# A two-layer hybrid backbone: table products on VectorE, sign folded into the product, table stores on other queues

## The chip, the cores and the metric

The kernel runs on one core of a Trainium2 chip. The metric is device microseconds (us) of one execution. Lower is better. Three runs of the kernel before gave 2425.04, 2426.26 and 2430.54 us, a median of 2426.26 us.

## The reference, cut to what matters

The model has two layers. Each runs a SwiGLU feed-forward block, four parallel token mixers on one normalised input, and a second feed-forward block; each block is normalised and modulated by vectors that come from a conditioning input. All of it is float32, over 256 latent and 256 context tokens of 1024 channels, with a hidden width of 2816.

```python
def swiglu(h, w1, w3, w2):
    return (jax.nn.silu(h @ w1) * (h @ w3)) @ w2

# one of the four mixers: a complex diagonal state space model, per group of 16 channels, 64 states
a_re, a_im, bb_re, bb_im = s5_discretize(lam_re[dr], lam_im[dr], log_dt[dr], b_re[dr], b_im[dr])
x_ctx = complex_scan(a_re, a_im, einsum('gpn,blgn->blgp', bb_re, ug_ctx), ..., None, rev)
x_lat = complex_scan(a_re, a_im, ..., (x_ctx[0][:, end], x_ctx[1][:, end]), rev)
y_lat = y_lat + (einsum('gnp,blgp->blgn', c_re[dr], x_lat[0])
                 - einsum('gnp,blgp->blgn', c_im[dr], x_lat[1]))
```

The state space mixer depends on the layer's parameters in two ways: through powers of the complex decay `a`, and through products of these powers with `bb` (the input map) and `c` (the output map). The kernel works these products out once per layer, as tables, and keeps them in DRAM until the mixer reads them.

## The kernel before

**The main stream.** Nearly all matmuls are float32 made of three float32r matmuls (`mm3`, L345 to L347): high part times high part, high times low, low times high. A weight piece is 128 x 1024. `piece` (L323) loads it into `raw` by a DMA on SP's queue (L326); ScalarE copies it to the high part `whi` (L317), VectorE subtracts to give the low part `wlo` (L318). `raw` has three buffers, `whi` and `wlo` four each. In a feed-forward block `up` runs 24 matmuls of 128 x 512 on one piece. After every second piece `act` (L681 to L688) makes the activation: `t` on ScalarE, `gf` on VectorE (L686), `gh` on ScalarE (L687), `gl` on VectorE (L688).

**Beside it.** While a feed-forward block runs, two generators are stepped along, 0.6 steps to a weight piece (`pace`). One is `ada` (L401), the modulation vectors: it loads pieces `araw` into the same three `raw` buffers, and VectorE reduces them with two vectors `cr` (L424, four instructions to a piece). The other is `s5_tables` (L1252), the tables of one layer. The tables of layer 0 run beside the first block of layer 0 (some 75 to 420 us of the span), those of layer 1 beside the second block of layer 0 (some 1060 to 1340 us). They are read by the mixers, some 400 us and more after they are stored.

**The tables.** After 16-wide arithmetic on VectorE, a loop over direction `d` and half `hf` (4 turns, L1347) makes two complex products of 128 x 512: `v` (powers times `bb`) and `g` (powers times `c`), each by `cmul` (L1214), which is six `tensor_tensor` instructions. Both run on GpSimd, and so does one `tensor_scalar` that flips the sign of g[1] (L1364). The two `g` go to DRAM table G by DMAs on SP's queue (L1367). `turned` (L1336) transposes the `v` of the turn before on TensorE (L1341), four 128 x 128 blocks into a PSUM bank of tag "f" (3 buffers), has ScalarE copy it out as `s5vt` (L1342), and stores it to table V on SP's queue (L1343). Matmuls of `g` give table K (16 small stores, L1411), from which DRAM copies make W (8, L1414); rotations R (4, L1450) and Z (2, L1451) end the tables. All of these stores, too, are on SP's queue. The counts are for one layer.

**The order.** A tile scheduler fixes one order of instructions for each engine and each queue; `behind` gives the tables a later priority than the main stream. An engine, and SP's queue, goes through its instructions strictly in that order: one that waits holds up all behind it.

Of the kernel before, what the change touches and what calls it, by code (L numbers as in the profile page):

```python
# [11 lines left out]
ALU = mybir.AluOpType  # L12
# [4 lines left out]
D = 1024  # L17
# [169 lines left out]
class Kern:  # L187
# [1023 lines left out]
        return t  # L1211


    def cmul(self, o, x, y, t, eng=None):  # L1214

        e = eng or self.nc.vector
        e.tensor_tensor(t[0], x[0], y[0], op=ALU.mult)
        e.tensor_tensor(t[1], x[1], y[1], op=ALU.mult)
        e.tensor_tensor(o[0], t[0], t[1], op=ALU.subtract)
        e.tensor_tensor(t[0], x[0], y[1], op=ALU.mult)  # L1220
        e.tensor_tensor(t[1], x[1], y[0], op=ALU.mult)
        e.tensor_tensor(o[1], t[0], t[1], op=ALU.add)

    def exp_small(self, x, sm):

# [26 lines left out]
    def s5_tables(self, l):  # L1252
# [3 lines left out]
        nc, vec, act = self.nc, self.nc.vector, self.nc.scalar  # L1256
# [73 lines left out]

        ncim = self.u("s5nc")
        vec.tensor_scalar(ncim[:, :256], ct[:, 256:], -1.0, None, op0=ALU.mult)
        D = self.s5_dram[l]
        G, held = {}, []

        def turned(d, hf, v):  # L1336

            for ri in range(2):
                pt, vt = self.ps("s5vt", "f"), self.u("s5vt")
                for a in range(4):  # L1340
                    nc.tensor.transpose(pt[:, a * P : (a + 1) * P], v[ri][:, a * P : (a + 1) * P], self.ident)  # L1341
                act.copy(vt, pt)  # L1342
                nc.sync.dma_start(D["V"][d, ri, hf], vt)  # L1343
                yield


        for d in range(2):  # L1347
            for hf in range(2):
                o = slice(8 * d + 4 * hf, 8 * d + 4 * hf + 4)
                shp = [P, 4, 8, 16]  # L1350
                v4 = lambda t: t.rearrange("p (a j m) -> p a j m", a=4, j=8)
                bcv = lambda x: x[:, o].unsqueeze(2).to_broadcast(shp)

                def pwv(rev, lo):
                    w = [p[:, o, lo : lo + 8] for p in pw]
                    return [(x[:, :, ::-1] if rev else x).unsqueeze(3).to_broadcast(shp) for x in w]

                ta, tb = self.u("s5ta"), self.u("s5tb")
                v = [self.u("s5v"), self.u("s5v")]
                self.cmul([v4(x) for x in v], [bcv(x) for x in bb], pwv(d == 0, 0), (v4(ta), v4(tb)), nc.gpsimd)  # L1360
                yield
                g = [self.u("s5g"), self.u("s5g")]
                self.cmul([v4(x) for x in g], [bcv(x) for x in c3_], pwv(d == 1, 1), (v4(ta), v4(tb)), nc.gpsimd)
                nc.gpsimd.tensor_scalar(g[1], g[1], -1.0, None, op0=ALU.mult)  # L1364
                for ri in range(2):
                    G[d, ri, hf] = g[ri]
                    nc.sync.dma_start(D["G"][d, ri, hf], g[ri])  # L1367
                yield
                if held:
                    yield from turned(*held.pop())  # L1370
                held.append((d, hf, v))
# [4 lines left out]
        for ri in range(2):  # L1376
            t = self.u("s5bd")
# [9 lines left out]
        for hf in range(2):  # L1387
            ps = self.ps("s5k", "f")
            seen = set()

            def mm(o, d, ri, rhs, stop):
                for q in range(4):
                    r = rhs(q)
                    nc.tensor.matmul(ps[32 * q : 32 * q + 32, o : o + r.shape[-1]], bd[ri][:, 8 * d + 4 * hf + q], r,
                                     start=q not in seen, stop=stop, tile_position=(0, 32 * q), skip_group_check=True)
                    seen.add(q)

            for d in range(2):
                for ri in range(2):
                    lo, c = (0, 128) if d == 0 else (16, 0)  # L1400
                    mm(c, d, ri, lambda q: G[d, ri, hf][:, q * P + lo : q * P + lo + 112], ri == 1)
            for d in range(2):
                mm(112, d, 0, lambda q: c3_[0][:, 8 * d + 4 * hf + q], False)
                mm(112, d, 1, lambda q: ncim[:, (8 * d + 4 * hf + q) * 16 : (8 * d + 4 * hf + q) * 16 + 16], d == 1)
            kt = self.u("s5k")
            act.copy(kt[:, :240], ps[:, :240])
            vec.tensor_tensor(kt[:, 112:128], kt[:, 112:128], dsk[:, 16 * hf : 16 * hf + 16], op=ALU.add)
            for q in range(4):
                for par in range(2):
                    r = 32 * q + 16 * par  # L1410
                    nc.sync.dma_start(D["K"][:, 4 * hf + q, 240 * par : 240 * par + 240], kt[r : r + 16, :240])  # L1411
            yield
        for s in range(8):
            nc.sync.dma_start(  # L1414
                D["W"][s], D["K"].rearrange("m a (b j) -> m (a b) j", b=2)[:, :, 16 * (7 - s) : 16 * (7 - s) + 128])

        rt = [sm("r8") for i in range(4)]
# [10 lines left out]
        for d in range(2):  # L1428
# [18 lines left out]
            vec.tensor_copy(zv, m8[:, o].unsqueeze(2).to_broadcast([P, 8, 64]))  # L1447
            vec.memset(zv[:, :, 0:1], 0.0)
            for i in range(2):
                nc.sync.dma_start(D["R"][d, i], rot[i])  # L1450
            nc.sync.dma_start(D["Z"][d], z)  # L1451

    def s5_in(self, l, H, tag):
        nc, vec, act, mm = self.nc, self.nc.vector, self.nc.scalar, self.nc.tensor.matmul
# [363 lines left out]
```

## Time and profile before

| | before |
|---|---|
| median of three runs | 2426.26 us |
| the profiled execution | 2430.84 us |
| its span, first to last instruction | 2429.1 us |
| TensorE busy (PE) | 2278.5 us, 94% |
| VectorE busy (DVE) | 1641.2 us, 68% |
| ScalarE busy (ACT) | 902.7 us, 37% |
| GpSimd busy (POOL) | 166.4 us, 7% |
| mean granted TensorE clock | 0.972 |

Times inside the trace are us from the span's start. An engine's row gives start, duration, engine, line, operation, output and input; a bracket gives the idle time before it and what ended that. A row of SP (SPq) is a DMA's issue, not the transfer. "PE idle" means no matmul ran. The digits that give the granted clock are shares of full speed: 1.00 is 2.4 GHz, and in a stretch at half it is 1.2 GHz.

### The profile page before, as it was taken

The numbers are of one execution on the slowest core, as the hardware profiler recorded it, in microseconds if no ns is written. First come the engines' busy times: TensorE is split into PE (matmuls) and PEld (weight loads), VectorE is DVE, ScalarE is ACT, GpSimd is POOL, SyncE is SP. The second block draws the span as 40 slices with busy tenths as digits, with TensorE's granted clock in tenths as the row PEclk, the third lists the DMA queues.
The fourth block names the chain that finished last, engine by engine and source line by source line (L and its number), as shares of the span: only waits on it lengthen the run. The fifth ranks groups of instructions, "written<-read, shape, count | busy, mean of one in ns | idle before, by whom it ended". The sixth has DMA issues, their size and how long they took to land.

```text
span 2429.1 us, 39327 instructions
## 1 busy us (share of the span) xinstructions
PE 2278.5 (94%) x15428; PEld 1923.3 (79%) x15428; DVE 1641.2 (68%) x3929; ACT 902.7 (37%) x1551; POOL 166.4 (7%) x144
## 2 busy tenths in 40 slices
PE   7969989999999999988799999999998999998997
PEld 4757878987667777887677898888898887898997
DVE  5876566766565565799665558868757787678554
ACT  3313323363443323442222233323234664345443
POOL 0093000000000000006510000000000000000000
PEclk9989999999999999999899999999998999998999
DMA  7526454232441242233454423656542332354663
GB/s 237 180 90 183 155 170 156 73 94 77 132 161 41 86 150 83 79 122 120 149 166 158 135 86 117 204 177 196 173 139 81 109 109 69 122 187 134 186 184 114
DMA packets 111226, 326.84 MB, mean 135 GB/s; under 512 B 16256, under 2 KB 23168, under 8 KB 111040
## 3 DMA queue, kind: packets, MB, share of 16 engines
q1 hardware_dynamic: 109024, 320.65, 42.8%
q10 hardware_dynamic: 2016, 3.67, 0.5%
q8 instruction: 121, 1.98, 0.3%
q14 instruction: 65, 0.53, 0.1%
HBM read 311.20 MB, written 15.17 MB: 134 GB/s over the span
## 4 chain that ended last, share of the span: by engine, by line
PE 73%; DVE 14%; DMA 6%; ACT 3%; issue 2%; POOL 2%; SPq 0%; DVEq 0%; ACTq 0%; POOLq 0%
PE h L345 8%; PE h L347 8%; PE h L346 8%; PE y L345 5%; PE y L347 5%; PE y L346 5%; PE pj L345 5%; PE pj L347 5%; PE pj L346 5%; DMA araw<-in_w_adaT_dram 3%; DVE wlo L318 3%; DVE aj L424 2%; DMA raw<-in_ffn_dram 2%; PE s L841 2%; DVE araw L424 1%
## 5 line engine op out<-in xcount | busy, mean ns | idle before, releaser
L317 ACT CAST whi<-raw 128x1024 fp32r<-128x1024 f32 x402 | 421.1, 1050 | 843.0 <-DMA raw<-in_ffn_dram 308.8
L318 DVE TENSOR_TENSOR wlo<-raw,whi 128x1024 fp32r<-128x1024 f32 x402 | 499.5, 1245 | 302.9 <-ACT whi L317 300.3
L347 PE MATMUL h<-hh,wlo 128*128 128x512 f32 (+1 forms) x1472 | 529.8, 361 | 22.1 <-DVE wlo L318 22.1
L345 PE MATMUL h<-hh,whi 128*128 128x512 f32 (+1 forms) x1472 | 531.2, 362 | 16.8 <-DVE gf L686 11.2
L346 PE MATMUL h<-hl,whi 128*128 128x512 f32 (+1 forms) x1472 | 528.3, 360 | 0.0
L347 PEld LDWEIGHTS h<-hh,wlo 128*128 128x128 f32 x1472 | 283.4, 193 | 67.7 <-DVE wlo L318 24.7
L345 PEld LDWEIGHTS h<-hh,whi 128*128 128x128 f32 x1472 | 284.1, 193 | 62.0 <-issue 12.1
L346 PEld LDWEIGHTS h<-hl,whi 128*128 128x128 f32 x1472 | 284.0, 193 | 39.2
L345 PE MATMUL y<-gh,whi 128*128 128x256 f32 (+1 forms) x902 | 290.3, 322 | 2.6 <-ACT t L685 2.6
L347 PE MATMUL y<-gh,wlo 128*128 128x256 f32 (+1 forms) x902 | 290.8, 323 | 0.0
L346 PE MATMUL y<-gl,whi 128*128 128x256 f32 (+1 forms) x902 | 290.5, 322 | 0.0
L345 PE MATMUL pj<-hh,whi 128*128 128x256 f32 (+1 forms) x800 | 276.5, 348 | 3.3 <-ACT hh L565 2.7
L347 PE MATMUL pj<-hh,wlo 128*128 128x256 f32 (+1 forms) x800 | 274.5, 345 | 3.5 <-DVE wlo L318 3.5
L346 PE MATMUL pj<-hl,whi 128*128 128x256 f32 (+1 forms) x800 | 275.4, 346 | 0.0
L345 PEld LDWEIGHTS y<-gh,whi 128*128 128x128 f32 x902 | 171.7, 190 | 15.7 <-ACT t L685 2.8
L346 PEld LDWEIGHTS y<-gl,whi 128*128 128x128 f32 x902 | 171.7, 190 | 13.0
L347 PEld LDWEIGHTS y<-gh,wlo 128*128 128x128 f32 x902 | 171.7, 190 | 12.8
L345 PEld LDWEIGHTS pj<-hh,whi 128*128 128x128 f32 x800 | 154.1, 194 | 23.6 <-issue 5.2
L347 PEld LDWEIGHTS pj<-hh,wlo 128*128 128x128 f32 x800 | 153.9, 193 | 23.6 <-DVE wlo L318 4.8
L346 PEld LDWEIGHTS pj<-hl,whi 128*128 128x128 f32 x800 | 154.2, 193 | 18.4 <-issue 3.9
L424 DVE SCALAR_TENSOR_TENSOR aj<-araw,cr 128x512 f32<-128x512 f32 x112 | 89.8, 802 | 81.8 <-DMA araw<-in_w_adaT_dram 80.1
L687 ACT CAST gh<-gf 128x512 fp32r<-128x512 f32 (+1 forms) x88 | 49.8, 565 | 161.4 <-DVE gf L686 160.0
(391 smaller groups left out, 3188.3 us busy)
## 6 DMA issues: line engine op xcount, KB each, us to landing
raw<-in_ffn_dram SPq DMA_DIRECT2D x267, 512.0 KB, 3.8
araw<-in_w_adaT_dram SPq DMA_DIRECT2D x104, 512.0 KB, 4.1
raw<-in_win_dram SPq DMA_DIRECT2D x102, 512.0 KB, 3.7
araw<-in_w_ada_dram SPq DMA_DIRECT2D x24, 512.0 KB, 4.0
raw<-in_wout_dram SPq DMA_DIRECT2D x17, 512.0 KB, 3.5
raw<-in_wbr_dram SPq DMA_DIRECT2D x16, 512.0 KB, 3.7
araw<-in_w_ada_dram SPq DMA_DIRECT2D x22, 256.0 KB, 5.9
s5G<-s5g SPq DMA_DIRECT2D x16, 256.0 KB, 4.5
```

Of the source, the lines that this page charges most:

```text
L317: self.nc.scalar.copy(hi, src)
L318: self.nc.vector.tensor_tensor(lo, src, hi.bitcast(F32), op=ALU.subtract)
L345: mm(ps, wh, xh, start=start, stop=False, skip_group_check=True)
L346: mm(ps, wh, xl, start=False, stop=False, skip_group_check=True)
L347: mm(ps, wl, xh, start=False, stop=stop, skip_group_check=True)
L424: nc.vector.scalar_tensor_tensor(w if v else junk, w, 1.0, S[v], op0=ALU.mult, op1=ALU.mult, accum_out=t[:, 2 * op + i, v : v + 1])
L687: nc.scalar.copy(gh[:, a:b], gf[:, a:b])
L841: nc.tensor.matmul(s[:, :w], q[:, j * P : (j + 1) * P], k[:, :w], start=True, stop=True)
```

## The change

`cmul` takes a further operand `nxi`, the negated imaginary part; with it the last product is written with its sign flipped, by a subtraction in place of the addition, so that the separate sign change is no longer needed. The negated part exists already as `ncim`. The `v` and `g` products run on VectorE. The stores of G, K, W, R and Z are issued by GpSimd, those of V by ScalarE right behind its own copy.

```diff
--- before.py
+++ after.py
@@ -1211,15 +1211,18 @@
         return t
 
 
-    def cmul(self, o, x, y, t, eng=None):
+    def cmul(self, o, x, y, t, eng=None, nxi=None):
 
         e = eng or self.nc.vector
         e.tensor_tensor(t[0], x[0], y[0], op=ALU.mult)
         e.tensor_tensor(t[1], x[1], y[1], op=ALU.mult)
         e.tensor_tensor(o[0], t[0], t[1], op=ALU.subtract)
         e.tensor_tensor(t[0], x[0], y[1], op=ALU.mult)
-        e.tensor_tensor(t[1], x[1], y[0], op=ALU.mult)
-        e.tensor_tensor(o[1], t[0], t[1], op=ALU.add)
+        e.tensor_tensor(t[1], x[1] if nxi is None else nxi, y[0], op=ALU.mult)
+        if nxi is None:
+            e.tensor_tensor(o[1], t[0], t[1], op=ALU.add)
+        else:
+            e.tensor_tensor(o[1], t[1], t[0], op=ALU.subtract)
 
     def exp_small(self, x, sm):
 
@@ -1330,6 +1333,7 @@
 
         ncim = self.u("s5nc")
         vec.tensor_scalar(ncim[:, :256], ct[:, 256:], -1.0, None, op0=ALU.mult)
+        nci = ncim[:, :256].rearrange("p (a m) -> p a m", m=16)
         D = self.s5_dram[l]
         G, held = {}, []
 
@@ -1340,7 +1344,7 @@
                 for a in range(4):
                     nc.tensor.transpose(pt[:, a * P : (a + 1) * P], v[ri][:, a * P : (a + 1) * P], self.ident)
                 act.copy(vt, pt)
-                nc.sync.dma_start(D["V"][d, ri, hf], vt)
+                act.dma_start(D["V"][d, ri, hf], vt)
                 yield
 
 
@@ -1357,14 +1361,13 @@
 
                 ta, tb = self.u("s5ta"), self.u("s5tb")
                 v = [self.u("s5v"), self.u("s5v")]
-                self.cmul([v4(x) for x in v], [bcv(x) for x in bb], pwv(d == 0, 0), (v4(ta), v4(tb)), nc.gpsimd)
+                self.cmul([v4(x) for x in v], [bcv(x) for x in bb], pwv(d == 0, 0), (v4(ta), v4(tb)))
                 yield
                 g = [self.u("s5g"), self.u("s5g")]
-                self.cmul([v4(x) for x in g], [bcv(x) for x in c3_], pwv(d == 1, 1), (v4(ta), v4(tb)), nc.gpsimd)
-                nc.gpsimd.tensor_scalar(g[1], g[1], -1.0, None, op0=ALU.mult)
+                self.cmul([v4(x) for x in g], [bcv(x) for x in c3_], pwv(d == 1, 1), (v4(ta), v4(tb)), None, bcv(nci))
                 for ri in range(2):
                     G[d, ri, hf] = g[ri]
-                    nc.sync.dma_start(D["G"][d, ri, hf], g[ri])
+                    nc.gpsimd.dma_start(D["G"][d, ri, hf], g[ri])
                 yield
                 if held:
                     yield from turned(*held.pop())
@@ -1408,10 +1411,10 @@
             for q in range(4):
                 for par in range(2):
                     r = 32 * q + 16 * par
-                    nc.sync.dma_start(D["K"][:, 4 * hf + q, 240 * par : 240 * par + 240], kt[r : r + 16, :240])
+                    nc.gpsimd.dma_start(D["K"][:, 4 * hf + q, 240 * par : 240 * par + 240], kt[r : r + 16, :240])
             yield
         for s in range(8):
-            nc.sync.dma_start(
+            nc.gpsimd.dma_start(
                 D["W"][s], D["K"].rearrange("m a (b j) -> m (a b) j", b=2)[:, :, 16 * (7 - s) : 16 * (7 - s) + 128])
 
         rt = [sm("r8") for i in range(4)]
@@ -1447,8 +1450,8 @@
             vec.tensor_copy(zv, m8[:, o].unsqueeze(2).to_broadcast([P, 8, 64]))
             vec.memset(zv[:, :, 0:1], 0.0)
             for i in range(2):
-                nc.sync.dma_start(D["R"][d, i], rot[i])
-            nc.sync.dma_start(D["Z"][d], z)
+                nc.gpsimd.dma_start(D["R"][d, i], rot[i])
+            nc.gpsimd.dma_start(D["Z"][d], z)
 
     def s5_in(self, l, H, tag):
         nc, vec, act, mm = self.nc, self.nc.vector, self.nc.scalar, self.nc.tensor.matmul
```

By the built programs, VectorE has 3569 rows and had 3473: 96 products of 128 x 512, 48 in each layer. GpSimd loses these 96 and 8 sign changes, and gains the DMA issues; what it still computes is the clearing of tiles. SP has 680 rows and had 730.

The first place is SP's queue in layer 0, at the first two turns of the loop (`raw` and `araw` are weight pieces, `s5g` the products on their way to table G). Before:

```order
L326 DMA raw_1325<-in_ffn_dram 128x1024
L1367 DMA s5G_90<-s5g_1063 128x512
L1367 DMA s5G_90<-s5g_1064 128x512
L326 DMA raw_1356<-in_ffn_dram 128x1024
L420 DMA araw_1362<-in_w_adaT_dram 128x1024
L1367 DMA s5G_90<-s5g_1197 128x512
L1367 DMA s5G_90<-s5g_1198 128x512
L326 DMA raw_1409<-in_ffn_dram 128x1024
L420 DMA araw_1415<-in_w_adaT_dram 128x1024
```

Now:

```order
L326 DMA raw_1323<-in_ffn_dram 128x1024
L326 DMA raw_1354<-in_ffn_dram 128x1024
L420 DMA araw_1360<-in_w_adaT_dram 128x1024
L326 DMA raw_1407<-in_ffn_dram 128x1024
L420 DMA araw_1413<-in_w_adaT_dram 128x1024
L326 DMA raw_1454<-in_ffn_dram 128x1024
L326 DMA raw_1493<-in_ffn_dram 128x1024
```

The four stores have left SP's queue, and the loads that stood behind them follow one another directly.

The second place is VectorE at the same time, up to the first weight piece after the products have begun (`s5ta`, `s5tb` are the products' temporaries, `s5bb` and `s5c` the maps, `s5s` small tables; the piece's name ends in 1244 before and in 1242 now). Before:

```order
L1219 TENSOR_TENSOR s5s_659<-s5s_658 128x16
L1220 TENSOR_TENSOR s5s_658<-s5s_659 128x16
L1221 TENSOR_TENSOR s5s_658<-s5s_659 128x16
L688 TENSOR_TENSOR gl_1046<-gf_1044,gh_1045 128x512
L1222 TENSOR_TENSOR s5s_659<-s5s_658 128x16
L1217 TENSOR_TENSOR s5s_658<-s5s_659 128x16
L1218 TENSOR_TENSOR s5s_658<-s5s_659 128x16
L1219 TENSOR_TENSOR s5s_659<-s5s_658 128x16
L1220 TENSOR_TENSOR s5s_658<-s5s_659 128x16
L1221 TENSOR_TENSOR s5s_658<-s5s_659 128x16
L1222 TENSOR_TENSOR s5s_659<-s5s_658 128x16
L318 TENSOR_TENSOR wlo_1244<-raw_1241,whi_1243 128x1024
```

Now, from the first product on; the row ahead of it, a gl, stands twelve rows ahead of the part shown of before:

```order
L1217 TENSOR_TENSOR s5ta_977<-s5bb_922,s5s_658 128x512
L1218 TENSOR_TENSOR s5tb_978<-s5bb_922,s5s_659 128x512
L424 SCALAR_TENSOR_TENSOR aj_651,mod_3_642<-araw_1276,cr_645 128x512
L1219 TENSOR_TENSOR s5v_979<-s5ta_977,s5tb_978 128x512
L424 SCALAR_TENSOR_TENSOR araw_1276,mod_3_642<-araw_1276,cr_648 128x512
L1220 TENSOR_TENSOR s5ta_977<-s5bb_922,s5s_659 128x512
L1221 TENSOR_TENSOR s5tb_978<-s5bb_922,s5s_658 128x512
L424 SCALAR_TENSOR_TENSOR aj_651,mod_3_642<-araw_1276,cr_645 128x512
L1223 TENSOR_TENSOR s5v_980<-s5ta_977,s5tb_978 128x512
L686 TENSOR_TENSOR gf_1044<-t_1043,h_1018 128x512
L424 SCALAR_TENSOR_TENSOR araw_1276,mod_3_642<-araw_1276,cr_648 128x512
L318 TENSOR_TENSOR wlo_1242<-raw_1239,whi_1241 128x1024
```

The six instructions of the first `v` product stand among the main stream's; the 16-wide instructions stand later, and the piece's `wlo` comes before the second `gl`.

The third place is VectorE at the end of the tables of layer 0, where the second K tile is finished (`s5k`). The bracket lists the semaphores that a row waits for; those that begin with DMAHW belong to DMAs issued by SP or ScalarE, those with DMASW to DMAs issued by GpSimd. Before:

```order
L686 TENSOR_TENSOR gf_2451<-t_2450,h_2425 128x512 [waits Activation_49]
L1407 TENSOR_TENSOR s5k_2383<-s5k_2383,s5d_2041 128x16
L688 TENSOR_TENSOR gl_2453<-gf_2451,gh_2452 128x512 [waits Activation_49]
L1432 MEMSET s5rot_2499 128x8
L1433 MEMSET s5rot_2500 128x8 [waits DMAHW4_49,DMAHW3_49,DMAHW5_49,DMAHW2_49,DMAHW6_49,DMAHW1_49,DMAHW0_49]
```

Now:

```order
L318 TENSOR_TENSOR wlo_2714<-raw_2711,whi_2713 128x1024 [waits DMAHW6_49,PE_49,Activation_49]
L686 TENSOR_TENSOR gf_2447<-t_2446,h_2421 128x512 [waits DMASW1_49,Activation_49]
L1410 TENSOR_TENSOR s5k_2379<-s5k_2379,s5d_2037 128x16 [waits DMASW6_49]
L688 TENSOR_TENSOR gl_2449<-gf_2447,gh_2448 128x512 [waits DMASW4_49,DMASW3_49,DMASW5_49,DMASW2_49,DMASW6_49,DMASW1_49,DMASW7_49,DMASW0_49,Activation_49]
L1435 MEMSET s5rot_2495 128x8 [waits PE_49]
```

The `gl` now waits for all eight of GpSimd's semaphores: its buffer is the one that the first K tile leaves. A memset that now stands a few rows later (s5rot_2729) waits for the eight in the same way.

## Rows read from the trace of the kernel before

**Rows 1.** The page, part 1: busy us, share of the span, instructions.

```profile
PE 2278.5 (94%) x15428; PEld 1923.3 (79%) x15428; DVE 1641.2 (68%) x3929; ACT 902.7 (37%) x1551; POOL 166.4 (7%) x144
```

**Rows 2.** Timeline, PE: start, duration, instruction, [idle before <- releaser].

```profile
163.16 1.48 PE L1341 MATMUL s5vt<-cst,s5v 128*128 128x128 f32 x12
186.96 1.09 PE L1341 MATMUL s5vt<-cst,s5v 128*128 128x128 f32 x4 [22.32 <-ACT s5vt L1342]
187.70 0.78 PE L345 MATMUL h<-hh,whi 128*128 128x512 f32 x1
...
313.34 0.76 PE L345 MATMUL h<-hh,whi 128*128 128x512 f32 x1 [4.86 <-DVE gf L686]
...
1145.02 0.80 PE L347 MATMUL h<-hh,wlo 128*128 128x512 f32 x1 [5.92 <-DVE wlo L318]
...
1188.95 1.09 PE L1341 MATMUL s5vt<-cst,s5v 128*128 128x128 f32 x4 [10.93 <-ACT s5vt L1342]
```

**Rows 3.** Windows: length, busy time and instructions of each engine, clock, DMA share, GB/s.

```profile
120.00:165.00 45.00, 40.63 (x182) 32.70 (x181) 36.15 (x60) 7.86 (x11) 41.05 (x29) 1.00 0.26 78
165.00:200.00 35.00, 13.04 (x48) 10.73 (x49) 22.27 (x36) 8.92 (x12) 19.63 (x15) 0.66 0.51 161
...
1165.00:1205.00 40.00, 29.07 (x121) 23.84 (x120) 26.23 (x41) 11.06 (x15) 14.12 (x9) 0.82 0.52 162
```

**Rows 4.** Timeline, ACT, at the first transposes.

```profile
166.16 1.04 ACT L317 CAST whi<-raw 128x1024 fp32r<-128x1024 f32 x1 [9.19 <-DMA raw<-in_ffn_dram]
...
185.28 1.04 ACT L317 CAST whi<-raw 128x1024 fp32r<-128x1024 f32 x1 [7.82 <-DMA raw<-in_ffn_dram]
186.24 0.58 ACT L1342 COPY s5vt<-s5vt 128x512 f32<-128x512 f32 x1
```

**Rows 5.** Timeline, SP's queue: start, time to the end of the last issue merged, DMA.

```profile
135.47 5.86 SPq L1367 DMA_DIRECT2D s5G<-s5g  x2
...
155.18 7.07 SPq L1367 DMA_DIRECT2D s5G<-s5g  x2
162.35 0.38 SPq L326 DMA_DIRECT2D raw<-in_ffn_dram  x1
...
325.17 3.87 SPq L1411 DMA_DIRECT2D s5K<-s5k  x8
...
337.53 4.36 SPq L1411 DMA_DIRECT2D s5K<-s5k  x8
...
1144.99 6.42 SPq L326 DMA_DIRECT2D raw<-in_ffn_dram  x2
```

**Rows 6.** Groups by line, DVE, 60 to 110 us, ahead of the products.

```profile
L688 DVE TENSOR_TENSOR gl<-gf,gh 128x512 fp32r<-128x512 f32 x4 | 2.7, 686 | 0.0
```

**Rows 7.** Groups by line, DVE, 121 to 181 us, beside GpSimd's products.

```profile
L318 DVE TENSOR_TENSOR wlo<-raw,whi 128x1024 fp32r<-128x1024 f32 x6 | 9.8, 1625 | 0.0
L424 DVE SCALAR_TENSOR_TENSOR aj<-araw,cr 128x512 f32<-128x512 f32 x7 | 8.7, 1244 | 15.1 <-DMA araw<-in_w_adaT_dram 15.1
...
L1219 DVE TENSOR_TENSOR s5s<-s5s 128x16 f32<-128x16 f32 x3 | 3.5, 1160 | 0.1
```

**Rows 8.** Groups by line, POOL, whole span: one of the products' twelve groups of eight.

```profile
L1222 POOL TENSOR_TENSOR s5g<-s5ta,s5tb 128x512 f32<-128x512 f32 x8 | 13.0, 1623 | 2.3 <-DMA s5V<-s5vt 1.8
```

**Rows 9.** Timeline, DVE.

```profile
123.65 0.68 DVE L688 TENSOR_TENSOR gl<-gf,gh 128x512 fp32r<-128x512 f32 x1
...
140.27 1.23 DVE L318 TENSOR_TENSOR wlo<-raw,whi 128x1024 fp32r<-128x1024 f32 x1
...
338.12 0.69 DVE L688 TENSOR_TENSOR gl<-gf,gh 128x512 fp32r<-128x512 f32 x1 [0.66 <-ACT gh L687]
...
346.75 0.07 DVE L1432 MEMSET s5rot<- 128x8 f32 x1
```

**Rows 10.** DMA issues: count, KB each, median us from issue to landing.

```profile
raw<-in_ffn_dram SPq DMA_DIRECT2D x267, 512.0 KB, 3.8
...
s5K<-s5k SPq DMA_DIRECT2D x32, 15.0 KB, 2.5
```

## The prediction

> **What bounds the kernel now.** The page comes first: TensorE is busy 94% of the span [rows 1], so a gain has to come out of the 6% in which it stands, or be nothing. The next view is the timeline of TensorE, read for its idle brackets. The two longest in the stretches where the tables are made are at the same code: the transposes of `v`. Three groups of four go into the three free PSUM banks (1.48 us), then the fourth group waits 22.32 us in layer 0 and 10.93 us in layer 1 for ScalarE to copy the first bank out [rows 2]. Two shorter waits in the same stretches are for VectorE: 5.92 us for a `wlo` and 4.86 us for a `gf` [rows 2]. The windows show what it comes to: of the 35 us from 165, TensorE works 13.04, at 0.66 of its clock; of the 40 us from 1165, 29.07 at 0.82 [rows 3].
>
> Why is ScalarE late with a copy of 0.58 us? Its own timeline says: it stands in casts (`whi`) whose `raw` has not landed, 9.19 us ahead of one and 7.82 us ahead of the last, and the copy runs right behind that, at 186.24 [rows 4]. ScalarE is in order, so the transposes wait for weight loads. And why are loads late? SP's queue stands at two G stores from 135.47 for 5.86 us and at two more from 155.18 for 7.07 us, since the `g` they store is not computed yet; a load goes out right behind them, at 162.35 [rows 5]. In layer 1 the scheduler put fewer stores in the way, but two `raw` issues take 6.42 us, waiting for a buffer that `wlo` frees late [rows 5].
>
> The last view is VectorE by line, ahead of the products and beside them. A 128 x 512 instruction with two SBUF inputs takes 686 ns ahead [rows 6]. Beside GpSimd's products the same size takes 1244 ns (L424), `wlo` 1625 ns against 1.23 us when alone, and a 16-wide instruction 1160 ns [rows 7, 9]. So three things meet: late stores block SP, GpSimd slows VectorE, and VectorE frees buffers late.
>
> **The change part by part.** *Products.* 96 instructions go from GpSimd to VectorE. One group of them takes 1623 ns each on GpSimd [rows 8]; on VectorE the row of that size says 686 ns [rows 6], so a turn's 12 take 8.2 us in place of some 19. The bounds: 0.69 us, or 1.62 us if they ran no faster there. I take 0.69, since that row is the same engine, size and kind. For a layer that adds 48 x 0.69 = 33 us to VectorE. What it takes away, in 121 to 181 alone: 6 x 0.40 for `wlo`, 14 x 0.56 for L424 (seven shown, seven alike), and about 1 us for each of the slow 16-wide instructions, of which one group of three is shown [rows 7]: some 2.4 + 7.8 + 8 = 18 us, with more beyond 181. VectorE's total is thus near unchanged, a few microseconds up, at 68% of the span [rows 1]. What changes is when things are done.
>
> *The first `wlo`.* In the order now, eleven rows of at most 0.69 us stand between the `gl` that starts at 123.65 and the next `wlo`; it starts by 123.65 + 12 x 0.69 = 131.9, in place of 140.27 [rows 6, 9]: 8.4 us sooner. Going down VectorE's new order in the same way, the next pieces' `wlo` end at about 137, 144, 150, 155 and 161. TensorE needs 24 x 40.63 / 182 = 5.4 us for a piece [rows 3], so VectorE stays a piece or two ahead of it, and TensorE comes to the transposes about 161, not 163.16 [rows 2].
>
> *The stores.* SP's queue loses them, so a load now waits for its buffer alone. The piece that ScalarE casts right ahead of the first copy gets the buffer that is freed at 161: 161.3 + 0.38 of issue + 3.8 of landing [rows 5, 10] = 165.5, cast 1.04, copy from 166.5. From the copy's start to the next piece before was 187.70 - 186.24 = 1.46 us [rows 2, 4], so that piece starts at 168.0; I take 168.5. **Layer 0 gains 187.7 - 168.5 = 19 us**; the stall at the transposes is cut from 22.3 to some 5 us, not removed. The clock gives nothing here: after the wait of 4.86 us too the matmul takes 0.76 us [rows 2], so a stall of 5 us also ends at the lower level.
>
> *Layer 1*, by the same walk: the late `wlo` comes some 13 us sooner, which removes the 5.92 us stall, and the copy can start near 1166.5, so that the transposes' last group stands at 1167.2, not 1188.95 [rows 2]: 21.7 us. I take **21**. Bounds for both layers: 8 us in sum, if only these two early `wlo` count (5.92 + about 2) and the rest waits on; 54, if the waits of all four rows go (44.0 [rows 2]) and TensorE's 13.04 and 29.07 us at 0.66 and 0.82 run at full clock (4.4 + 5.2 [rows 3]).
>
> *The wait of 4.86 us.* There `gf` stands on VectorE behind an L424 whose `araw` is late. In the new order it stands ahead of the `wlo` that follows, still behind four L424. 0 to 5 us; I take 0.
>
> *Stores on GpSimd.* Hidden as long as nobody needs their buffers soon. The G stores, 8 a layer, have no reader near. The K stores have one: in the new order a `gl` waits until the eight stores of the first K tile have landed, and a memset for the eight of the second. Before, the first eight went out at 325.17 and this `gl` ran at 338.12, 13 us later; the second eight at 337.53 and the memset at 346.75, 9.2 us later [rows 5, 9]. The trace of before has no store issued by GpSimd. Bounds for one: 3.87 / 8 = 0.48 us as on SP [rows 5], or 2.5 us, a whole landing [rows 10], if each were done before the next. Eight at 0.48 and a landing make 6.4 us: hidden in both places. At c us each, the memset waits when 8c + 2.5 is over 9.2, so from c = 0.84. Behind that memset on VectorE stand the `wlo` of the next piece and so TensorE, which has a piece or two in hand (5 us and more). I take c = 1, nearer to the issue than to the landing: 1.3 us late, hidden, cost 0. In a layer the memset costs 8c + 2.5 - 9.2 - 5 and the `gl` 8c + 2.5 - 13 - 5, so both layers 32c - 54: at 2.5 us 26 us in all.
>
> A page speaks against this part: the Trainium skill, "DMA: Bandwidth & Descriptors", section "Anatomy of one DMA — SWDGE (gpsimd) path", gives about 2.0 us fixed for a DMA issued there. Taken as the time from one issue to the next, that is c = 2.0, 10 us less of gain and 2396 us; taken as a latency that overlaps, it changes nothing. No run here shows which.
>
> *V stores on ScalarE.* 16 issues of about 0.4 us each [rows 5], behind a copy that is already done: ScalarE is busy 37% [rows 1]. 0 to 6 us, if each held TensorE up; I take 0.
>
> *Sign.* 8 instructions of GpSimd go, nothing comes. 0.
>
> Sum: 19 + 21 + 0 - 0 = 40 us. On the profiled execution that is 2430.8 - 40 = 2391; it lies 4.6 us above the median of the runs, so for the median 2426.3 - 40 = **2386 us**.
>
> **The rivals.**
> *A, VectorE becomes the bound.* Where products crowd (four turns in some 110 us beside `ada`), TensorE stands for `wlo` in many short waits. For it: VectorE was busy 36.15 of the 45 us from 120 [rows 3] and gets 33 us in each layer. Against it: the slowing that it loses is as large. The stalls at the transposes would be cut by half: gain 20, **2406 us**.
> *B, all the way.* With loads never late, the copy runs at once, both stalls vanish, the clock stays up: gain 54, **2372 us**. Against it: the cast ahead of the copy still waits for a buffer.
> *C, the stores were not the cause.* SP's wait would then have been idle time only, and the loads would have come no sooner, since buffers were not free. Gain 5.92 + 2 = 8, **2418 us**. The trace speaks against it: a load goes out 0.1 us after the stores end [rows 5]. The Trainium skill, "DMA: Bandwidth & Descriptors", section "Issuing engines are not separate DMA queues", says that issuing from several engines saves only the issue time; by that rule this case is the right one, but the row shows 7.07 us for two issues, which is a wait and not issue time.
> *D, slower.* GpSimd's stores come out one by one and VectorE stands at the four places where it needs their buffers, with a `wlo` and TensorE behind it. The price is 32c - 54 us as worked out above; it decides from c = 2.95, where it eats the 40. At c = 3.2 it is 48 - 40 = 8, **2434 us**; if the gain is only the 20 of A, c = 2.6 gives the same. For it: a landing takes 2.5 us even from SP [rows 10], and no store of GpSimd's is in the trace. Against it: SP got eight out in 3.87 us [rows 5], so the transfers overlap.
> *E, nothing.* The stalls turn up again elsewhere, 2426.
>
> **How the numbers follow.** Forecast 0.46, A 0.18, B 0.16, C 0.08, D 0.07, E 0.05. The forecast's own spread is some 10 us each way. From 2364 to 2412 the range holds the forecast, A and nearly all of B, some 8 in 10. About 0.2% (4.9 us) is what a measurement of this kernel can tell from no change. Faster: forecast, A, B, C = 0.88; same 0.05; slower 0.07.
>
> **What would show it.** In the profile after: the wait of the fourth group of transposes near 5 us in both layers, the copy about 166 and 1167; SP with no row of over 2 us at a store; L424 at 0.69 us in all tables stretches; the stall of 5.92 us gone; no wait of VectorE for K stores over 5 us. It is wrong if VectorE's products take over 0.8 us, if TensorE shows new waits for `wlo` (A), if the fourth group still waits over 12 us (C), or if a `gl` or memset stands for DMAs of GpSimd's (D).

## The result, and the profile after

The changed kernel runs in 2369.2 us, the median of four runs (2363.3 to 2373.3). The kernel before has a median of 2426.9 us in its four. The ratio is 0.9754, with a 95% interval of 0.9737 to 0.9771, so the gain is some 60 us (56 to 64 by the interval). The forecast was 2386 us, a gain of 40, with a range of 2364 to 2412: the time lies inside, near the lower end. The profiled execution took 2369.64 us, with a span of 2367.8 and a mean clock of 0.982 (before: 0.972).

The engines' row answers [rows 1]:

```profile
PE 2267.1 (96%) x15428; PEld 1915.7 (81%) x15428; DVE 1635.8 (69%) x4025; ACT 903.0 (38%) x1551; POOL 53.3 (2%) x116
```

VectorE has 96 instructions more, and is busy 5.4 us less. The groups by line for VectorE, 121 to 181 us, answer [rows 6, 7]:

```profile
L318 DVE TENSOR_TENSOR wlo<-raw,whi 128x1024 fp32r<-128x1024 f32 x9 | 11.0, 1219 | 0.0
L424 DVE SCALAR_TENSOR_TENSOR aj<-araw,cr 128x512 f32<-128x512 f32 x11 | 7.6, 687 | 7.6 <-DMA araw<-in_w_adaT_dram 7.4
...
L1220 DVE TENSOR_TENSOR s5ta<-s5bb,s5s 128x512 f32<-128x512 f32 x3 | 2.1, 689 | 0.0
```

L424 is down from 1244 to 687 ns and `wlo` from 1625 to 1219; a product takes 689 ns. At 0.689 us the 96 products add 66 us. Since the total still fell by 5.4, the slowing beside GpSimd had cost VectorE some 71 us.

TensorE's timeline answers [rows 2], the windows answer [rows 3]:

```profile
162.45 1.47 PE L1345 MATMUL s5vt<-cst,s5v 128*128 128x128 f32 x12
166.81 0.66 PE L1345 MATMUL s5vt<-cst,s5v 128*128 128x128 f32 x4 [2.90 <-ACT s5vt L1346]
167.31 0.50 PE L345 MATMUL h<-hh,whi 128*128 128x512 f32 x1
...
288.50 0.39 PE L345 MATMUL h<-hh,whi 128*128 128x512 f32 x1
...
1108.58 0.39 PE L347 MATMUL h<-hh,wlo 128*128 128x512 f32 x1
...
1132.96 0.66 PE L1345 MATMUL s5vt<-cst,s5v 128*128 128x128 f32 x4 [1.59 <-ACT s5vt L1346]
1133.46 0.50 PE L345 MATMUL h<-hh,whi 128*128 128x512 f32 x1
```

```profile
120.00:165.00 45.00, 41.38 (x180) 33.90 (x180) 41.96 (x101) 10.81 (x14) 2.29 (x4) 0.96 0.43 139
165.00:200.00 35.00, 33.19 (x147) 27.29 (x148) 25.68 (x49) 13.04 (x19) 1.08 (x2) 1.00 0.61 192
...
1130.00:1170.00 40.00, 38.41 (x178) 31.84 (x177) 30.22 (x55) 16.00 (x23) 1.08 (x2) 1.00 0.58 186
```

The two long waits at the transposes are 2.90 and 1.59 us (22.32 and 10.93 before), and the two shorter ones, for a `gf` and a `wlo`, have no bracket any more. Waits for a `wlo` came to 2.3 and 11.1 us in the two stretches before; now there is none. Behind the transposes the clock stays at 1.00. The 0.96 of the first window comes from a dip well ahead of them: from 125 to 130 us, behind a wait of 2.74 us for a `gf`, the granted clock is 0.75.

Since the order of the weight matmuls (L345 to L347) is nearly the same in both traces, they can be lined up one by one. The table gives the start of the same matmul in both, and how much earlier it is now:

| place | before, us | after, us | earlier by, us |
|---|---|---|---|
| layer 0, first matmul behind the transposes | 187.70 | 167.31 | 20.4 |
| the same piece, 12 matmuls on | 192.81 | 170.16 | 22.7 |
| behind the wait for `gf` | 313.34 | 288.50 | 24.8 |
| 12 matmuls on | 318.60 | 291.22 | 27.4 |
| end of the first mixers | 981.10 | 951.08 | 30.0 |
| layer 1, behind the wait for `wlo` | 1145.02 | 1108.58 | 36.4 |
| 59 matmuls on | 1168.30 | 1121.96 | 46.3 |
| first matmul behind the transposes | 1189.69 | 1133.46 | 56.2 |
| past the last wait of these tables | 1318.40 | 1253.87 | 64.5 |
| end of the span | 2429.1 | 2367.8 | 61.3 |

All of it but a few microseconds arises in the two stretches in which tables are made. The table rests on one trace of each kernel, and traces differ by an offset: at 60 us, ahead of all tables, this one is 0.7 us ahead of the one before, and a second trace of the changed kernel 4.8. So a gain is read from one place to the next, not from one entry.

SP's queue and the queue of GpSimd answer [rows 5]:

```profile
148.08 6.02 SPq L326 DMA_DIRECT2D raw<-in_ffn_dram  x2
...
161.68 2.28 SPq L326 DMA_DIRECT2D raw<-in_ffn_dram  x2
```

```profile
300.35 3.85 POOL L1414 DMA_DIRECT2D s5K<-s5k  x8 [48.53 <-issue]
310.62 3.82 POOL L1414 DMA_DIRECT2D s5K<-s5k  x8 [6.41 <-DVE s5k L1410]
```

SP issues loads alone in these stretches, and stands at no store. GpSimd gets eight K stores out in 3.85 us, as SP did in 3.87.

### The profile page after: what moved, and what is told of

Same layout as the page of the kernel before. It is cut to its first block, busy times and chain, and to the rows that moved or that the text cites. A ratio compares the mean times of both kernels' runs of the same rounds, so it can differ in the third digit from the quotient of the medians.

```text
span 2367.8 us, 39296 instructions
## 1 busy us (share of the span) xinstructions
PE 2267.1 (96%) x15428; PEld 1915.7 (81%) x15428; DVE 1635.8 (69%) x4025; ACT 903.0 (38%) x1551; POOL 53.3 (2%) x116
## 4 chain that ended last, share of the span: by engine, by line
PE 84%; DVE 10%; ACT 3%; DMA 2%; issue 1%; SPq 0%; DVEq 0%; ACTq 0%
PE h L345 11%; PE h L347 11%; PE h L346 11%; PE y L345 6%; PE y L347 6%; PE y L346 6%; PE pj L345 5%; PE pj L347 5%; PE pj L346 5%; PE s L841 2%; DVE wlo L318 2%; DMA araw<-in_w_adaT_dram 1%; PE od L868 1%; ACT whi L317 1%; PE tk L347 1%
## 5 line engine op out<-in xcount | busy, mean ns | idle before, releaser
L317 ACT CAST whi<-raw 128x1024 fp32r<-128x1024 f32 x402 | 421.2, 1050 | 810.4 <-DMA raw<-in_ffn_dram 282.9
L318 DVE TENSOR_TENSOR wlo<-raw,whi 128x1024 fp32r<-128x1024 f32 x402 | 490.7, 1222 | 287.6 <-ACT whi L317 285.5
L345 PE MATMUL h<-hh,whi 128*128 128x512 f32 (+1 forms) x1472 | 528.1, 360 | 12.2 <-DVE gf L686 5.0
L347 PE MATMUL h<-hh,wlo 128*128 128x512 f32 (+1 forms) x1472 | 526.0, 359 | 8.7 <-DVE wlo L318 8.7
L345 PEld LDWEIGHTS h<-hh,whi 128*128 128x128 f32 x1472 | 281.8, 192 | 57.6 <-issue 5.3
L347 PEld LDWEIGHTS h<-hh,wlo 128*128 128x128 f32 x1472 | 281.8, 192 | 51.1 <-DVE wlo L318 8.8
L345 PE MATMUL y<-gh,whi 128*128 128x256 f32 (+1 forms) x902 | 290.4, 322 | 2.5 <-ACT t L685 2.5
L347 PE MATMUL y<-gh,wlo 128*128 128x256 f32 (+1 forms) x902 | 291.0, 323 | 0.0
L345 PE MATMUL pj<-hh,whi 128*128 128x256 f32 (+1 forms) x800 | 276.8, 348 | 3.3 <-ACT hh L565 2.7
L347 PE MATMUL pj<-hh,wlo 128*128 128x256 f32 (+1 forms) x800 | 274.5, 345 | 4.3 <-DVE wlo L318 4.3
L345 PEld LDWEIGHTS y<-gh,whi 128*128 128x128 f32 x902 | 171.7, 190 | 15.7 <-ACT t L685 2.7
L347 PEld LDWEIGHTS y<-gh,wlo 128*128 128x128 f32 x902 | 171.7, 190 | 12.9
L347 PEld LDWEIGHTS pj<-hh,wlo 128*128 128x128 f32 x800 | 154.2, 194 | 24.7 <-DVE wlo L318 4.9
L345 PEld LDWEIGHTS pj<-hh,whi 128*128 128x128 f32 x800 | 154.2, 194 | 23.6 <-issue 5.2
L424 DVE SCALAR_TENSOR_TENSOR aj<-araw,cr 128x512 f32<-128x512 f32 x112 | 77.0, 687 | 55.9 <-DMA araw<-in_w_adaT_dram 55.7
L586 DVE TENSOR_TENSOR sqa<-sqa,sq 128x256 f32<-128x256 f32 (+1 forms) x154 | 71.6, 493 | 49.9 <-ACT sq L588 49.3
```

The lines of the kernel that those rows point to most:

```text
L317: self.nc.scalar.copy(hi, src)
L318: self.nc.vector.tensor_tensor(lo, src, hi.bitcast(F32), op=ALU.subtract)
L345: mm(ps, wh, xh, start=start, stop=False, skip_group_check=True)
L347: mm(ps, wl, xh, start=False, stop=stop, skip_group_check=True)
L424: nc.vector.scalar_tensor_tensor(w if v else junk, w, 1.0, S[v], op0=ALU.mult, op1=ALU.mult, accum_out=t[:, 2 * op + i, v : v + 1])
L586: nc.vector.tensor_tensor(out[k][:, a:b], out[k][:, a:b], t[:, a:b], op=ALU.add)
```

## The experiments

Ratios are to the kernel before, run on the same chip in the same set, with a 95% interval.

| kernel | products on | stores on | ratio | interval |
|---|---|---|---|---|
| the change | VectorE | GpSimd, ScalarE | 0.9754 | 0.9737 to 0.9771 |
| the change, again | VectorE | GpSimd, ScalarE | 0.9759 | 0.9741 to 0.9777 |
| products alone | VectorE | SP | 0.9767 | 0.9752 to 0.9782 |
| products alone, again | VectorE | SP | 0.9764 | 0.9747 to 0.9781 |
| stores alone | GpSimd | GpSimd, ScalarE | 0.9962 | 0.9945 to 0.9978 |
| G stores alone | GpSimd | G on GpSimd, others SP | 0.9987 | 0.9970 to 1.0003 |
| sign alone | GpSimd | SP | 0.9962 | 0.9945 to 0.9978 |
| change + multiplications on GpSimd | VectorE | as the change | 0.9998 | 0.9988 to 1.0008 |
| change + one-input operations on GpSimd | VectorE | as the change | 0.9853 | 0.9829 to 0.9876 |
| change + memsets on GpSimd | VectorE | as the change | 0.9779 | 0.9764 to 0.9793 |
| before, products mostly memsets | GpSimd (memsets) | SP | 0.9823 | 0.9802 to 0.9845 |
| change, copies on VectorE | VectorE | GpSimd | 0.9763 | 0.9741 to 0.9785 |

**The two halves of the change.** First the stores alone, with the products and the sign change back on GpSimd:

```diff
-                self.cmul([v4(x) for x in v], ..., (v4(ta), v4(tb)))
+                self.cmul([v4(x) for x in v], ..., (v4(ta), v4(tb)), nc.gpsimd)
...
-                self.cmul([v4(x) for x in g], ..., (v4(ta), v4(tb)), None, bcv(nci))
+                self.cmul([v4(x) for x in g], ..., (v4(ta), v4(tb)), nc.gpsimd)
+                nc.gpsimd.tensor_scalar(g[1], g[1], -1.0, None, op0=ALU.mult)
```

> Only the stores move (G, K, W, R, Z to GpSimd's queue, V to ScalarE's); the products and the sign change stay on GpSimd. Theory of the prediction (SP's queue, contention on VectorE and VectorE's order each take their part): SP no longer stands at a G store, but L424 stays at 1.2 us and more beside the products and the first late wlo still starts near 140; the copy of s5vt comes 8 to 15 us sooner in layer 0 and little sooner in layer 1. Gain 10 to 25 us, 2402 to 2417. If the SP queue were all: the gain of the whole change, 2365 to 2375. If only VectorE's contention counted: 2421 to 2427, no change.

Then the products alone, with every store back on SP's queue (`act.dma_start` and `nc.gpsimd.dma_start` in the tables become `nc.sync.dma_start`):

> Only the products and the folded sign move to VectorE; all stores stay on SP's queue. Theory of the prediction: the stores wait less, since g is ready sooner, but a load still stands behind a store now and then; gain 30 to 45 us, 2382 to 2397, with the wait of the fourth group of transposes at 5 to 10 us. If VectorE's contention is all: 2365 to 2375, as the whole change. If the SP queue is all: near 2427.

The stores alone gave 0.9962, some 9 us (5 to 13). The products alone gave 0.9767, 57 us (53 to 60). The theory on record had put 10 to 25 and 30 to 45, and missed both. For the products the branch that came true is the one in which VectorE's contention is all; for the stores that branch said no change, and 9 us are more than that. So the products carry nearly the whole gain by themselves. With stores alone VectorE's groups and the transposes read (121 to 181 us, and TensorE's timeline):

```profile
L318 DVE TENSOR_TENSOR wlo<-raw,whi 128x1024 fp32r<-128x1024 f32 x7 | 14.1, 2009 | 0.0
L424 DVE SCALAR_TENSOR_TENSOR aj<-araw,cr 128x512 f32<-128x512 f32 x8 | 9.3, 1161 | 12.7 <-DMA araw<-in_w_adaT_dram 12.7
```

```profile
175.26 1.09 PE L1345 MATMUL s5vt<-cst,s5v 128*128 128x128 f32 x4 [14.67 <-ACT s5vt L1346]
```

SP is free there, `wlo` is still slow, at 2009 ns, and the wait is still 14.67 us (22.32 before). With the products alone, SP's queue and the transposes read:

```profile
143.99 0.33 SPq L1370 DMA_DIRECT2D s5G<-s5g  x1
146.42 0.33 SPq L326 DMA_DIRECT2D raw<-in_ffn_dram  x1
147.56 0.33 SPq L420 DMA_DIRECT2D araw<-in_w_adaT_dram  x1
148.89 0.33 SPq L1370 DMA_DIRECT2D s5G<-s5g  x1
```

```profile
159.91 0.66 PE L1345 MATMUL s5vt<-cst,s5v 128*128 128x128 f32 x4 [2.44 <-ACT s5vt L1346]
```

The G stores are still in SP's queue, but no load goes out right behind one: a store's `g` is there in time, since a product no longer takes as long. The longest that SP stands at one from 120 to 200 us is 2.2 us.

**Do the moved stores add anything?** Both kernels again in one set, with the G stores alone as a third (`nc.gpsimd.dma_start(D["G"]...)` in the kernel before, nothing else):

> The changed kernel again, beside the next one on the same chip. 0.974 to 0.977 of the kernel before.

> Products and sign on VectorE, all stores on SP's queue, again, beside the changed kernel. If the moved stores add nothing once the products are on VectorE: the same ratio within 0.001. If they still free SP's queue: the changed kernel is 3 to 8 us faster than this one.

> The kernel before with the G stores alone on GpSimd's queue; VectorE, TensorE and ScalarE have the order of before. If the 9 us of all stores moved come from the G stores, at which SP stands: 5 to 12 us faster than before, 2415 to 2422. If they come from the V, K and W stores: 0 to 3 us.

The change gave 0.9759 and the products alone 0.9764: no difference that can be measured. The G stores alone gave 0.9987, 3 us, with an interval from 7 us faster to 1 us slower: no gain clear of the noise. This is the run that shows what SP's waits at the G stores were worth. The first fence is SP's queue, the second what it waited for from 150 to 156 us (us in total, times, longest), the third VectorE, the fourth TensorE, all with the G stores off SP:

```profile
154.38 0.33 SPq L326 DMA_DIRECT2D raw<-in_ffn_dram  x1
```

```profile
SPq L326 <- DVE wlo L318: 8.6, 1, 8.6
```

```profile
152.28 2.07 DVE L318 TENSOR_TENSOR wlo<-raw,whi 128x1024 fp32r<-128x1024 f32 x1
```

```profile
181.18 1.09 PE L1341 MATMUL s5vt<-cst,s5v 128*128 128x128 f32 x4 [14.73 <-ACT s5vt L1342]
...
1180.38 1.09 PE L1341 MATMUL s5vt<-cst,s5v 128*128 128x128 f32 x4 [14.23 <-ACT s5vt L1342]
```

The load goes out at 154.38, right behind the slow `wlo` that ends at 154.35: it waits for its buffer where it had waited for a store. It is the load that went out at 162.35 before [rows 5], so the store had held it up by 8 us; without the store it still waits 8.6 us, for the `wlo`. The wait at the transposes fell by 7.6 us in layer 0 and rose by 3.3 in layer 1. Lined up as in the table above, this trace gains some 7 us in layer 0 (the whole change: 27) and next to nothing in layer 1. All stores moved gave 9 us and the G stores 3; the intervals overlap, so what the other stores give stays open.

**Is it GpSimd's reading?** The changed kernel, with GpSimd kept busy where the products were. VectorE, SP, ScalarE and TensorE keep the order of the changed kernel.

```diff
+                jk = self.u("s5j")
+                for _ in range(6):
+                    nc.gpsimd.tensor_tensor(v4(jk), bcv(bb[0]), pwv(d == 0, 0)[0], op=ALU.mult)
                 yield
                 g = [self.u("s5g"), self.u("s5g")]
...
+                for _ in range(6):
+                    nc.gpsimd.tensor_tensor(v4(jk), bcv(bb[0]), pwv(d == 0, 0)[0], op=ALU.mult)
```

> The changed kernel, with 48 more multiplications of 128 x 512 with two SBUF inputs a layer on GpSimd, at the places where the products were, into a tile that nobody reads: 12 to a turn, their results unused. The order of instructions on VectorE, SP, ScalarE and TensorE is that of the changed kernel. If GpSimd's reading slows VectorE and that is what TensorE waits for: L424 back at 1.2 us and more beside them, wlo at 1.6 us, and 30 to 60 us of the gain of 58 lost, 2400 to 2430 (VectorE also carries the real products here). If the queue of stores is what counts: 2365 to 2375.

With `nc.gpsimd.memset(jk, 0.0)` in its place:

> The same kernel with 48 memsets of 128 x 512 a layer on GpSimd in place of the 48 multiplications, so GpSimd is busy at these places but reads nothing of SBUF. If it is the reading that slows VectorE: L424 stays at 0.69 us and the time is that of the changed kernel, 2362 to 2375. If any work of GpSimd's slows it: 5 us or more above 2375.

With one input, `nc.gpsimd.tensor_scalar(v4(jk), bcv(bb[0]), -1.0, None, op0=ALU.mult)`:

> The changed kernel with 48 multiplications of one SBUF input by a constant a layer on GpSimd, 128 x 512, into a tile that nobody reads. If one read is enough to slow VectorE's instructions with two SBUF inputs: L424 at 1.1 us and more beside them, 2400 to 2430, as with two inputs (2428). If it takes two inputs: near the 2374 of the kernel with memsets.

The multiplications take all of the gain away (0.9998), the memsets next to none of it (0.9779). VectorE carries its own products here as well, so this loss need not be the same as the price of GpSimd's reading in the kernel before. The memsets are the run to compare it with. Groups by line, 121 to 181 us, VectorE and GpSimd, with the multiplications; then the window:

```profile
L424 DVE SCALAR_TENSOR_TENSOR aj<-araw,cr 128x512 f32<-128x512 f32 x7 | 9.6, 1366 | 0.0
L318 DVE TENSOR_TENSOR wlo<-raw,whi 128x1024 fp32r<-128x1024 f32 x6 | 9.0, 1501 | 0.0
...
L686 DVE TENSOR_TENSOR gf<-t,h 128x512 f32<-128x512 f32 x3 | 2.0, 677 | 0.0
```

```profile
L1372 POOL TENSOR_TENSOR s5j<-s5bb,s5s 128x512 f32<-128x512 f32 x14 | 20.0, 1427 | 1.0
```

```profile
120.00:165.00 45.00, 32.31 (x128) 25.54 (x126) 45.00 (x58) 6.13 (x8) 28.21 (x23) 0.89 0.27 88
```

VectorE is busy for all of the 45 us, and TensorE falls from 41.38 to 32.31 with no store in SP's queue. The same groups with memsets:

```profile
L424 DVE SCALAR_TENSOR_TENSOR aj<-araw,cr 128x512 f32<-128x512 f32 x11 | 7.6, 689 | 7.9 <-DMA araw<-in_w_adaT_dram 7.8
```

```profile
L1367 POOL MEMSET s5j<- 128x512 f32 x12 | 6.4, 530 | 0.6
```

A memset is shorter than a multiplication (530 against 1427 ns), so this run alone leaves open whether it is the reading or the time that GpSimd is busy; the kernel with memsets as long as the products, below, answers that. And with one input:

```profile
L424 DVE SCALAR_TENSOR_TENSOR aj<-araw,cr 128x512 f32<-128x512 f32 x10 | 8.2, 823 | 4.9 <-DMA araw<-in_w_adaT_dram 4.9
```

```profile
L1372 POOL TENSOR_SCALAR s5j<-s5bb 128x512 f32<-128x512 f32 x17 | 28.8, 1694 | 1.3
```

One input is between: L424 at 823 ns, some 24 us of the gain gone (0.9853 - 0.9754). Neither branch of that expectation came true; GpSimd's work slows VectorE when it reads, and this operation with two inputs slows it more than this one with one, although the one-input operation is the longer (1694 against 1427 ns).

**The late stores without the slowing.** The kernel before with its stores on SP, and GpSimd's products mostly turned into memsets of the same total length. It leaves out five of the six instructions of each product.

```diff
         e.tensor_tensor(t[0], x[0], y[0], op=ALU.mult)
+        if eng is not None:
+            for q in (t[1], o[0], t[0], t[1], o[1]):
+                for _ in range(3):
+                    e.memset(q, 0.5)
+            return
...
-                nc.gpsimd.tensor_scalar(g[1], g[1], -1.0, None, op0=ALU.mult)
+                for _ in range(3):
+                    nc.gpsimd.memset(g[1], 0.5)
```

> The kernel before with its stores on SP's queue, and of each complex product on GpSimd only the first multiplication left; the other five instructions, and the sign change, are three memsets of 128 x 512 each, so the tables hold no products (this part of the computation is left out). GpSimd is busy about as long for a turn as before, some 19 us (3 x 0.53 for one of 1.2 to 1.8), so the G stores come as late and SP's queue stands at them as before, but GpSimd reads SBUF a sixth as often. VectorE has no product. Theory now (GpSimd's reading slows VectorE, the stores' waits cost little by themselves): 35 to 55 us faster, 2372 to 2392, with L424 near 0.75 us and SP still standing 4 us and more at a G store. Theory of the prediction (the loads are late since SP's queue stands): 5 to 20 us faster, 2407 to 2422.

0.9823, 43 us faster, inside what was expected of the slowing. GpSimd's memsets lie almost without a gap from 121 to 181 us, and one of VectorE's two L424 groups stays at 690 ns there; the other, at 777, holds a few that ran beside a multiplication that is left:

```profile
L424 DVE SCALAR_TENSOR_TENSOR araw<-araw,cr 128x512 f32<-128x512 f32 x12 | 8.3, 690 | 0.3
```

So it is the reading, and not that GpSimd is busy, that slows VectorE. SP's queue and TensorE:

```profile
133.87 0.38 SPq L420 DMA_DIRECT2D araw<-in_w_adaT_dram  x1
140.68 0.33 SPq L1373 DMA_DIRECT2D s5G<-s5g  x1
141.10 0.38 SPq L326 DMA_DIRECT2D raw<-in_ffn_dram  x1
```

```profile
164.74 0.63 PE L1346 MATMUL s5vt<-cst,s5v 128*128 128x128 f32 x4 [1.72 <-ACT s5vt L1347]
...
1146.38 1.09 PE L1346 MATMUL s5vt<-cst,s5v 128*128 128x128 f32 x4 [9.72 <-ACT s5vt L1347]
```

SP issues nothing from 134.25 to 140.68 and a load follows the store at once, as before the change; and yet the wait at the transposes in layer 0 is 1.72 us. In layer 1 it is 9.72. By the same lining up, layer 0 gains 25 us up to 400 us, against 27 with the whole change, and some 13 of the 16 us that are missing are missing in layer 1. SP's waits there, from 1100 to 1150 us, and a `wlo` beside one of the multiplications that are left:

```profile
SPq L326 <- DVE wlo L318: 16.1, 5, 5.8
...
SPq L1373 <- POOL s5g L1370: 0.3, 1, 0.3
```

```profile
1132.83 2.08 DVE L318 TENSOR_TENSOR wlo<-raw,whi 128x1024 fp32r<-128x1024 f32 x1
```

SP stands at G stores for 0.3 us in all there, so late G stores do not explain it. What remains is the sixth of the reading that is left, or VectorE's order, which is that of before; this run doesn't tell these two apart.

**The sign alone.** The kernel before with `nxi` given to the second product, on GpSimd, and the sign change dropped:

> The kernel before with the sign folded into the last product alone: eight instructions of 1.8 us less on GpSimd, all else in its place. The second store of a turn is ready 1.8 us sooner. Either theory: 0 to 4 us faster, 2423 to 2427; if the wait at the G stores is what delays the loads, 4 to 10 us faster.

0.9962, some 9 us. That is more than the 0 to 4 of either theory, and lies in the branch that was put down for the case that the wait at the G stores delays the loads, 4 to 10 us. The G stores alone, which take that wait away, gave 3 us (at most 7), so the branch is neither shown nor excluded. Dropping the sign change also takes 8 x 1.83 = 14.6 us of reading off GpSimd, of some 154 in all, which at the price of the whole (60 us) is 5 or 6; the interval (5 to 13 us) holds that. So the sign may have gained by less reading, by earlier stores, or by both.

**One step further.** Copies out of PSUM on VectorE, so that they don't stand behind a cast:

```diff
-                act.copy(vt, pt)
-                act.dma_start(D["V"][d, ri, hf], vt)
+                vec.tensor_copy(vt, pt)
+                nc.gpsimd.dma_start(D["V"][d, ri, hf], vt)
```

> The changed kernel, with the copies of the transposes out of PSUM on VectorE in place of ScalarE, and their stores issued by GpSimd. The copies no longer stand behind a cast that waits for a load, so the waits of 2.9 and 1.6 us of the fourth group should go; each copy adds 0.6 us to VectorE, 16 in all. If VectorE has room: 2 to 6 us faster than the changed kernel, 2363 to 2367, ratio to the kernel before 0.973 to 0.975. If VectorE bounds there: the same or up to 8 us slower.

0.9763, not to be told from the change; the 2 to 6 us that were put down for the case that VectorE has room are not there. TensorE has no wait at the transposes any more, but one of about the same length right behind them, for the `t` that ScalarE makes after its cast:

```profile
166.45 0.53 PE L345 MATMUL h<-hh,whi 128*128 128x512 f32 x1 [2.50 <-ACT t L685]
```

## Why the prediction came out as it did

*What bounds the kernel.* Right to look at TensorE's waits in the tables stretches: they held the gain. Wrong in the next step, which took the stores in SP's queue as the cause of the late loads. A load that goes out 0.1 us behind a store [rows 5] shows that the store was the last thing that it waited for. It does not show what it would have waited for next. With the G stores gone it came 8 us sooner and then stood for a buffer that a slow `wlo` freed (154.38 behind 154.35), and the kernel gained at most 7 us of the 60. Of the "three things" named there, the last two carried nearly all, and the second is the cause of the third: GpSimd slows VectorE, and VectorE frees buffers late. That 2369 lies in the range is no proof of the path that led to 2386: the gain was a third too small, and part of it was put down to the stores.

*Products.* 0.69 us was forecast for one, 0.689 measured. VectorE's total was to stay near unchanged: 1641.2 and 1635.8. Right; but the working took this as a wash, and looked for the gain in the loads.

*The first `wlo`.* Its start by 131.9 at the latest was forecast. It starts at 130.54, as VectorE's timeline shows:

```profile
130.54 1.22 DVE L318 TENSOR_TENSOR wlo<-raw,whi 128x1024 fp32r<-128x1024 f32 x1
```

*The stores, layer 0.* The copy from 166.5 and the next piece at 168.0 were forecast. ScalarE's timeline, which answers [rows 4], has the copy at 166.18, and the piece starts at 167.31:

```profile
165.23 1.05 ACT L317 CAST whi<-raw 128x1024 fp32r<-128x1024 f32 x1 [5.87 <-DMA raw<-in_ffn_dram]
166.18 0.58 ACT L1346 COPY s5vt<-s5vt 128x512 f32<-128x512 f32 x1
```

The sum holds, 20.4 us for 19, because the walk had both halves of the change in it, and in part by luck: TensorE came to the transposes at 162.45, not at 161, and waited 2.90 us, not 5. Its heading was wrong. In the trace with the products alone the same piece is 27.3 us earlier than before, of which 6.6 stand already at 60 us: 20.7 without the moved stores, against 20.4 - 0.7 = 19.7 with them.

*The clock.* "The clock gives nothing here" failed. The wait that is left is 2.90 us, not 5, and the matmul behind it takes 0.50 us, not 0.76 to 0.78. By the table the next 12 matmuls gain 2.3 us more in layer 0 (22.7 - 20.4), and the 12 behind the wait for `gf`, which is gone, 2.5 (27.4 - 24.8).

*The wait of 4.86 us* was taken at 0 of 0 to 5. It is gone. From 192.81 to 318.60, with the clock behind it and less what other small waits take back, the table gives 27.4 - 22.7 = 4.7 us.

*Layer 1.* 21 was forecast up to the transposes. It is 56.2 - 30.0 = 26.2, and 8.3 more to the end of these tables. The walk took account of one short wait ahead of the transposes, the 5.92 us, and of none behind, nor of the clock. TensorE's waits of before, from 1050 to 1340 us (us in total, times, longest), hold more:

```profile
PE h L347 <- DVE wlo L318: 11.1, 3, 5.9
PE h L345 <- DVE gf L686: 4.1, 1, 4.1
```

After the change they are none for a `wlo` and 2.2 us for a `gf`. Layer 1 is thus the term that was undersized most, by some 13 us with all that followed.

*Stores on GpSimd.* 1 us for an issue was forecast, between 0.48 and 2.5. It is 3.85 / 8 = 0.48 us, the lower end, so nothing waits for it: the memset that needs the second eight runs at 318.93, 4.5 us after they are out (310.62 + 3.82). The 2.0 us that the Trainium skill gives for such a DMA ("DMA: Bandwidth & Descriptors", "Anatomy of one DMA — SWDGE (gpsimd) path") is not the time from one issue to the next here.

*The rivals.* A: VectorE did not become the bound. In 120 to 165 it is busy 41.96 of 45 us, close to it, but TensorE works 41.38, and no wait for a `wlo` came up. B: its 2372 us is nearest to the result; both stalls shrank to under 3 us and the clock stayed up. C had most of the reason, that buffers were not free, though the one load did come 8 us sooner; its price was wrong, since it left out what the products give through these same buffers. The rule of the Trainium skill cited there, that issuing from several engines saves only the issue time ("DMA: Bandwidth & Descriptors", "Issuing engines are not separate DMA queues"), agrees with 0.9759 against 0.9764. The 7.07 us row that was held against it is a wait, and such waits had their price beside GpSimd's products: all stores moved gave 9 us (0.9962). D did not come near: c is 0.48.

## What to carry to other kernels

A queue that stands at one instruction shows the last of its waits; what a load waits for when that is gone has to be read separately, here the release of its buffer three loads back. Work given to an idle engine need not be free: here its reading slowed the busy one. So compare the durations of the busy engine's instructions ahead of the moved work and beside it, for each shape, before anything is said about hidden work. When a walk through a new order gives the right time, that alone does not say which part of the change gave it: half of the change, run alone, does.

## What was not expected of the hardware

Memsets of GpSimd's cost VectorE nothing (L424 at 689 and 690 ns), a one-input operation some 20% (823), a two-input one twice the time (1366). These are means from 121 to 181 us, in which not every L424 has GpSimd's work beside it. `gf`, which has one of its inputs in PSUM, keeps 675 to 681 ns in all these runs. The Trainium skill, "SBUF — State Buffer", section "SBUF: two separate sides", says that a VectorE instruction with two SBUF inputs and a GpSimd operation that reads SBUF shut each other out of a shared pair of ports for a whole instruction; the memset and `gf` rows agree, and that one input costs less than two, though it runs longer, is not in that sentence. A store of 256 KB landed in a median of 3.0 us from GpSimd's queue after the change and 4.5 us from SP's before, but the queue does not make that difference: with the products alone, the median from SP's queue is 2.9 us. The DMA issues of after, of before and of the products alone:

```profile
s5G<-s5g POOLq DMA_DIRECT2D x16, 256.0 KB, 3.0
```

```profile
s5G<-s5g SPq DMA_DIRECT2D x16, 256.0 KB, 4.5
```

```profile
s5G<-s5g SPq DMA_DIRECT2D x16, 256.0 KB, 2.9
```
